# Attention in a hybrid decoder layer: turning two steps behind the scores instead of one

## The chip, the cores and the metric

One core of a Trainium2 chip runs one layer of a decoder trunk in float32. The metric is the device time of one execution in microseconds (us), lower is better. TensorE is PE in the profile (its weight loads PEld), VectorE is DVE, ScalarE is ACT, GpSimd is POOL, and SyncE (SP) issues nearly all transfers.

## The reference

The layer normalises x (2048 rows of 1024), scales and shifts it by an adaptive modulation, projects it once, and feeds three token mixers: spatial gating, an mLSTM matrix memory, and stick-breaking attention. Their outputs are gated, concatenated, projected and added to x. The change lies in the attention, with 6 heads of 64 and blocks of 128 queries:

```python
z = jnp.einsum('bthd,bshd->bhts', qb, kb).astype(jnp.float32) * scale
strict = s_idx[None, :] < t_idx[:, None]
log_not = jnp.where(strict, jax.nn.log_sigmoid(-z), 0.0)
suffix = lax.cumsum(log_not, axis=3, reverse=True) - log_not
a = jnp.where(strict, jnp.exp(jax.nn.log_sigmoid(z) + suffix), 0.0)
outs.append(jnp.einsum('bhts,bshd->bthd', a.astype(vb.dtype), vb))
```

Each weight is sigmoid(z) times the product of all 1 - sigmoid(z) at later keys.

## The kernel before

**Blocks and passes.** The 16 query tiles of 128 rows are taken in three blocks of 5, 5 and 6. For each block the attention runs in three passes p, each of two heads. `c_proj` makes the pass's queries, keys and values (`Qst`, `Kst`, `Vst`), then `stick` yields the attention step by step, and `interleave` sets matmuls of the other projections (`bqk_proj`, `bg_proj`, `cz_proj`, `a_proj`; here "filler") between the steps by their cost. Behind the third pass comes `bv_proj` (tiles `pv`). After the last block an output stage reads everything back, runs the mLSTM and the output projection.

**A unit** is one query tile i, one head h and up to 512 keys from tile s0 on. It passes four functions. `front` (L372) makes the scores z with two matmuls (L378, L379); ACT evacuates them twice, sigmoid(-z) into `bb` (L383) and sigmoid(z) into `be` (L384); POOL masks the tile on the diagonal (L386, L388); VectorE scans `bb` from the right into running products (L391); and VectorE for every other unit, POOL for the rest, multiplies `be` by them (L395). `middle` (L399) turns `be` by up to four transposes on TensorE into the PSUM tile `at` (L406), ACT copies that into `aT` (L408), and VectorE subtracts the rounded copy to get the remainder (L409, here "the subtraction"). `back` (L413) multiplies by the values (L421, the products) and at a row's end adds the two halves (L425 on ACT, L427 on VectorE). `fin` (L431) folds two heads into a tile and stores it (L437 to L440). A scan takes its start from the scan of the unit before it in the same row (`carry`).

**Order.** The loop at the end of `stick` takes unit n's front, then the middle of unit n-1, the back of n-2, the fin of n-3:

```python
        for n in range(N + 3):
            for lag, fn in ((0, front), (1, middle), (2, back), (3, fin)):
                if 0 <= n - lag < N:
                    yield fn(units[n - lag])
```

This is the order in which the steps are handed to a scheduler, which then places every instruction on its engine's queue by priority (attention stands ahead of filler, `STK` = -30) and by its own estimate of when inputs are there. What it leaves is one fixed order per engine, and each engine works its queue in that order. There are 240 units.

**Tiles.** In SBUF the pool `stk` holds 4 tiles of `bb`, 3 of `be` and 3 of `aT` (4 KB a partition). `aT` also serves two tiles of x at the start (L120), `be` two rows of norm weights (L212). In PSUM the scores have 2 banks, `at` 2, the products 1, the projections 3.

Of the kernel before, what the change touches and what calls it, by code (L numbers as in the profile page):

```python
# [8 lines left out]
F32 = mybir.dt.float32  # L9
F32R = mybir.dt.float32r  # L10
# [7 lines left out]
P = 128  # L18
SEQ = 2048
NT = SEQ // P  # L20
D = 1024
# [11 lines left out]
def hybrid_block_kernel(ctx: ExitStack, tc: tile.TileContext, x, c, norm_g, w_ada, b_ada, w_in,  # L33
                        ga_v_norm, ga_ws, ga_bs, mb_conv_w, mb_conv_b, mb_b_i, mb_b_f, mb_h_norm,
                        sc_q_norm, sc_k_norm, w_out, out):
    nc = tc.nc
# [59 lines left out]
    stk = rs.enter_context(tc.tile_pool(name="stk", bufs=2, side="right"))  # L96
# [18 lines left out]
    def load_x(i, j, halves=None):  # L115
        if halves is None:
            if j % 4 < 2:
                xt = tmp.tile([P, D], F32, tag="xt", name=f"xt{i}")
            else:
                xt = stk.tile([P, D], F32, tag="aT", bufs=3, name=f"xt{i}")  # L120
            nc.sync.dma_start(xt, x[0, i * P:(i + 1) * P, :])
            xtiles[i] = [[xt], None]
        else:
            for hh in range(2):
                nc.sync.dma_start(halves[hh], x[0, i * P:(i + 1) * P, hh * 512:(hh + 1) * 512])
            xtiles[i] = [halves, None]
# [27 lines left out]
    def get_x(i, j):  # L154
        load_x(i, j % 2)
        rms_x(i)
        for hh in range(len(xtiles[i][0])):
            w = D // len(xtiles[i][0])
            mod_x(i, hh * w, (hh + 1) * w)
# [49 lines left out]
    brow = [stk.tile([P, 512], F32, tag="bb", bufs=4, name=f"brow{n}") for n in range(4)]  # L209
    for n in (2, 0, 3, 1):  # L210
        nc.gpsimd.memset(brow[n], 0.0)
    g_bc = [stk.tile([P, 512], F32, tag="be", bufs=3, name=f"g_bc{n}") for n in range(2)]  # L212

    def ada_load(half):
        for n, c0 in enumerate((1024 + 512 * half, 512 * half)):
# [43 lines left out]
    for j in range(NB0):  # L259
        halves = None  # L260
        if j == 4:
            halves = vg_halves(4)
        elif j == 5:
            halves = [t512(f"x5_{hh}") for hh in range(2)]
        load_x(j, j, halves)
        if j < 2:
            staged[j] = load_w(w_in[0], c_segs(0), j)
# [89 lines left out]
    def stick(p, t0, nb):  # L357
# [14 lines left out]
        def front(u):  # L372
            i, j, h, s0, s1 = u
            w = (s1 - s0) * P
            nm = f"{p}_{i}_{h}_{s0}"
            z = pz.tile([P, 512], F32, tag="z", name=f"z{nm}")
            kk = Kst[:, h, s0 * P:s1 * P]
            nc.tensor.matmul(z[:, :w], lhsT=Qst[:, j, 0, h, :], rhs=kk, start=True, stop=False)  # L378
            nc.tensor.matmul(z[:, :w], lhsT=Qst[:, j, 1, h, :], rhs=kk, start=False, stop=True)  # L379
            bb = stk.tile([P, 513], F32, tag="bb", bufs=4, name=f"bb{nm}")  # L380
            be = stk.tile([P, 512], F32, tag="be", bufs=3, name=f"be{nm}")
            nc.gpsimd.memset(bb[:, w:w + 1], 1.0)  # L382
            nc.scalar.activation(bb[:, :w], z[:, :w], AF.Sigmoid, scale=-1.0)  # L383
            nc.scalar.activation(be[:, :w], z[:, :w], AF.Sigmoid)  # L384
            if s1 == i + 1:
                nc.gpsimd.affine_select(out=bb[:, w - P:w], in_=bb[:, w - P:w], pattern=[[-1, P]],  # L386
                                        compare_op=ALU.is_gt, fill=1.0, base=0, channel_multiplier=1)
                nc.gpsimd.affine_select(out=be[:, w - P:w], in_=be[:, w - P:w], pattern=[[-1, P]],  # L388
                                        compare_op=ALU.is_gt, fill=0.0, base=0, channel_multiplier=1)
            rev = bb[:, 0:w + 1][:, ::-1]  # L390
            nc.vector.tensor_tensor_scan(rev, rev, rev, carry.get((i, h), 1.0), ALU.mult, ALU.bypass)  # L391
            carry[i, h] = bb[:, 0:1]
            eng = nc.gpsimd if len(st_count) % 2 else nc.vector
            st_count.append(0)
            eng.tensor_tensor(be[:, :w], be[:, :w], bb[:, 1:w + 1], ALU.mult)  # L395
            st[u] = [be, None]
            return 2 * w / 2.4

        def middle(u):  # L399
            i, j, h, s0, s1 = u  # L400
            nm = f"{p}_{i}_{h}_{s0}"
            be = st[u][0]
            nb_ = s1 - s0
            at = pat.tile([P, 4, P], F32, tag="at", name=f"at{nm}")
            for s in range(nb_):
                nc.tensor.transpose(at[:, s, :], be[:, s * P:(s + 1) * P], ident)  # L406
            aT = stk.tile([P, 4, 2, P], F32R, tag="aT", bufs=3, name=f"aT{nm}")
            nc.scalar.copy(aT[:, :nb_, 0, :], at[:, :nb_, :])  # L408
            nc.vector.tensor_tensor(aT[:, :nb_, 1, :], at[:, :nb_, :], aT[:, :nb_, 0, :].bitcast(F32), ALU.subtract)  # L409
            st[u][1] = aT  # L410
            return nb_ * 109
# [29 lines left out]
            return 430  # L441

        N = len(units)
        for n in range(N + 3):
            for lag, fn in ((0, front), (1, middle), (2, back), (3, fin)):
                if 0 <= n - lag < N:
                    yield fn(units[n - lag])

# [595 lines left out]
```

## Time and profile before

| | |
|---|---|
| median of 3 runs | 1482.28 us (1481.29 to 1483.16) |
| the profiled execution, its own time | 1480.27 us |
| its span, first to last instruction | 1478.5 us |
| mean granted TensorE clock | 0.982 of full speed |
| busy: PE, PEld | 1400.6 us, 1302.7 us |
| busy: DVE, ACT, POOL | 1025.1 us, 678.1 us, 647.3 us |
| DMA moved | 233.19 MB, mean 158 GB/s |

Busy time is what an engine spends in instructions. "Idle before" is time in which it stood still just ahead of an instruction, and the name behind the arrow is what ended that. Times of matmuls include a modelled end, so back-to-back matmuls overlap in the listing. All windows below are us from the span's start.

### The profile page before, as it was taken

Reading aid. Unit: us, or ns where it says so; the run is one execution under the profiler, and the core shown is the slowest. Engines: PE = TensorE matmul, PEld = TensorE weight load, DVE = VectorE, ACT = ScalarE, POOL = GpSimd, SP = SyncE. Lnnn points to the kernel's source line nnn. Section 1 sums busy time; section 2 is a strip of 40 time slices with the busy share of each in tenths; the row PEclk is TensorE's granted clock in tenths of the full one; section 3 lists DMA queues with packets and bytes.
Section 4 is the critical chain, followed back from the end, with each engine's and each line's share of the span. In section 5 each row is a group of like instructions: output and inputs, shape, how many; then the busy total and the mean of one; then the engine's idle time right before and its main releaser. Section 6 shows DMA issues by size and latency. Waiting matters only on the chain.

```text
span 1478.5 us, 24942 instructions
## 1 busy us (share of the span) xinstructions
PE 1400.6 (95%) x8468; PEld 1302.7 (88%) x8468; DVE 1025.1 (69%) x1778; ACT 678.1 (46%) x1656; POOL 647.3 (44%) x1140
## 2 busy tenths in 40 slices
PE   4999999889999999999999899999999978999998
PEld 3789999879999999988899799989999867888887
DVE  6796555586894566588698975778778888444443
ACT  3365444444464355446367655555455655211210
POOL 4463554573443433455233353433344336534442
PEclk9999999999999999999999999999999998999999
DMA  9866766657635534625332343303432524555551
GB/s 319 305 203 216 249 213 190 207 187 240 203 114 194 175 114 137 213 98 184 114 117 78 104 148 131 104 27 107 158 100 74 190 89 128 185 152 159 171 156 57
DMA packets 187103, 233.19 MB, mean 158 GB/s; under 512 B 22714, under 2 KB 160344, under 8 KB 186976
## 3 DMA queue, kind: packets, MB, share of 16 engines
q1 hardware_dynamic: 186752, 231.59, 48.1%
q8 instruction: 67, 1.10, 0.3%
q14 instruction: 60, 0.49, 0.1%
q0 software_dynamic: 224, 0.02, 0.0%
HBM read 159.24 MB, written 72.31 MB: 157 GB/s over the span
## 4 chain that ended last, share of the span: by engine, by line
PE 68%; DVE 16%; DMA 5%; issue 4%; POOL 3%; ACT 3%; SPq 1%; DVEq 0%; POOLq 0%; ACTq 0%
DVE bb L391 6%; PE av L421 5%; PE pc L296 4%; PE pc L298 4%; PE at L406 4%; PE pc L297 4%; PE po L957 4%; PE po L959 3%; PE po L958 3%; PE pg L298 3%; PE pg L297 3%; PE pg L296 3%; PE pb L465 2%; PE pb L464 2%; PE z L378 2%
## 5 line engine op out<-in xcount | busy, mean ns | idle before, releaser
L391 DVE TENSOR_TENSOR_SCAN bb<-bb,bb 128x513 f32<-128x513 f32 x144 | 194.1, 1348 | 24.9 <-ACT bb L383 23.8
L395 POOL TENSOR_TENSOR be<-be,bb 128x512 f32<-128x512 f32 (+3 forms) x120 | 133.0, 1108 | 148.3 <-DVE bb L391 69.2
L409 DVE TENSOR_TENSOR aT<-at,aT 128x512 fp32r<-128x512 f32 (+3 forms) x240 | 142.7, 597 | 31.5 <-ACT aT L408 30.5
L421 PE MATMUL av<-aT,Vst 128*128 128x256 f32 x816 | 146.4, 296 | 15.0 <-DVE aT L409 12.1
L408 ACT CAST aT<-at 128x512 fp32r<-128x512 f32 (+3 forms) x240 | 127.1, 530 | 70.3 <-PE at L406 67.4
L383 ACT ACTIVATE bb<-z 128x512 f32<-128x512 f32 (+3 forms) x240 | 130.3, 544 | 54.5 <-PE z L379 44.2
L421 PEld LDWEIGHTS av<-aT,Vst 128*128 128x128 f32 x816 | 120.5, 192 | 27.0 <-DVE aT L409 19.2
L296 PE MATMUL pc<-wr,hT 128*128 128x384 f32 (+1 forms) x384 | 136.8, 358 | 7.6 <-DVE hT L290 5.7
L406 PE MATMUL at<-ident,be 128*128 128x128 f32 x816 | 132.8, 277 | 9.6 <-DVE Qst L351 4.5
L298 PE MATMUL pc<-wr,hT 128*128 128x384 f32 (+1 forms) x384 | 135.5, 353 | 1.6 <-DVE hT L290 1.5
L297 PE MATMUL pc<-wr,hT 128*128 128x384 f32 (+1 forms) x384 | 134.0, 349 | 0.0
L384 ACT ACTIVATE be<-z 128x512 f32<-128x512 f32 (+3 forms) x240 | 132.1, 550 | 0.0
L406 PEld LDWEIGHTS at<-ident,be 128*128 128x128 f32 x816 | 99.2, 142 | 19.0 <-DVE aT L409 8.0
L957 PE MATMUL po<-wo,yT 128*128 128x512 f32 x256 | 105.0, 410 | 0.3 <-ACT yT L946 0.3
L958 PE MATMUL po<-wo,yT 128*128 128x512 f32 x256 | 102.3, 400 | 1.9 <-DVE wo L864 1.9
L391 DVE TENSOR_TENSOR_SCAN bb<-bb 128x129 f32<-128x129 f32 (+3 forms) x96 | 86.9, 905 | 23.5 <-POOL bb L386 16.3
L959 PE MATMUL po<-wo,yT 128*128 128x512 f32 x256 | 101.5, 400 | 0.0
L382 POOL MEMSET bb<- 128x1 f32 x240 | 24.2, 101 | 168.4 <-DVE bb L391 118.1
L378 PE MATMUL z<-Kst,Qst 128*128 128x512 f32 (+3 forms) x240 | 92.7, 387 | 1.7 <-ACT be L384 1.6
L466 PE MATMUL pb<-hT,wr 128*128 128x320 f32 (+1 forms) x288 | 91.9, 324 | 2.4 <-DVE wr L190 2.4
L464 PE MATMUL pb<-hT,wr 128*128 128x320 f32 (+1 forms) x288 | 93.1, 324 | 0.6 <-DMA wr<-w_d 0.6
L465 PE MATMUL pb<-hT,wr 128*128 128x320 f32 (+1 forms) x288 | 92.2, 322 | 0.0
(272 smaller groups left out, 3905.2 us busy)
## 6 DMA issues: line engine op xcount, KB each, us to landing
wr<-w_d SPq DMA_DIRECT2D x160, 384.0 KB, 5.6
w_d<-wr SPq DMA_DIRECT2D x80, 384.0 KB, 3.5
wad<-in_w_ada_dram SPq DMA_DIRECT2D x8, 1024.0 KB, 6.8
xo<-in_x_dram SPq DMA_DIRECT2D x16, 512.0 KB, 3.7
out_dram<-o SPq DMA_DIRECT2D x31, 256.0 KB, 2.9
xt<-in_x_dram SPq DMA_DIRECT2D x15, 512.0 KB, 3.5
st<-in_w_in_dram SPq DMA_DIRECT2D x60, 128.0 KB, 3.7
wr<-w_d SPq DMA_DIRECT2D x16, 392.0 KB, 6.0
```

The source lines that it names most:

```text
L296: nc.tensor.matmul(ps, lhsT=hT[:, 0, k, cols], rhs=wt[k][:, 0, :W], start=k == 0, stop=False)
L297: nc.tensor.matmul(ps, lhsT=hT[:, 0, k, cols], rhs=wt[k][:, 1, :W], start=False, stop=False)
L298: nc.tensor.matmul(ps, lhsT=hT[:, 1, k, cols], rhs=wt[k][:, 0, :W], start=False, stop=k == KT - 1)
L384: nc.scalar.activation(be[:, :w], z[:, :w], AF.Sigmoid)
L391: nc.vector.tensor_tensor_scan(rev, rev, rev, carry.get((i, h), 1.0), ALU.mult, ALU.bypass)
L395: eng.tensor_tensor(be[:, :w], be[:, :w], bb[:, 1:w + 1], ALU.mult)
L406: nc.tensor.transpose(at[:, s, :], be[:, s * P:(s + 1) * P], ident)
L409: nc.vector.tensor_tensor(aT[:, :nb_, 1, :], at[:, :nb_, :], aT[:, :nb_, 0, :].bitcast(F32), ALU.subtract)
L421: nc.tensor.matmul(flat(av), lhsT=Vst[:, s0 + s, h, :], rhs=flat(aT[:, s]), start=(s0 + s == i), stop=(s0 + s == 0))
L957: nc.tensor.matmul(po, lhsT=yT[:, 0, k, :], rhs=wo[k][:, 0, cs], start=k == 0, stop=False)
L958: nc.tensor.matmul(po, lhsT=yT[:, 0, k, :], rhs=wo[k][:, 1, cs], start=False, stop=False)
L959: nc.tensor.matmul(po, lhsT=yT[:, 1, k, :], rhs=wo[k][:, 0, cs], start=False, stop=k == KT - 1)
```

## The change

The middle of a unit is queued two steps behind its front, the back three, the fin four. The tags `be` and `aT` get a fourth tile each. To make room in SBUF the program's DMA scratch is set to 4096 bytes.

```diff
-                xt = stk.tile([P, D], F32, tag="aT", bufs=3, name=f"xt{i}")
+                xt = stk.tile([P, D], F32, tag="aT", bufs=4, name=f"xt{i}")
...
-    g_bc = [stk.tile([P, 512], F32, tag="be", bufs=3, name=f"g_bc{n}") for n in range(2)]
+    g_bc = [stk.tile([P, 512], F32, tag="be", bufs=4, name=f"g_bc{n}") for n in range(2)]
...
-            be = stk.tile([P, 512], F32, tag="be", bufs=3, name=f"be{nm}")
+            be = stk.tile([P, 512], F32, tag="be", bufs=4, name=f"be{nm}")
...
-            aT = stk.tile([P, 4, 2, P], F32R, tag="aT", bufs=3, name=f"aT{nm}")
+            aT = stk.tile([P, 4, 2, P], F32R, tag="aT", bufs=4, name=f"aT{nm}")
...
-        for n in range(N + 3):
-            for lag, fn in ((0, front), (1, middle), (2, back), (3, fin)):
+        for n in range(N + 4):
+            for lag, fn in ((0, front), (2, middle), (3, back), (4, fin)):
...
-    nc = _bacc.Bacc("TRN2", target_bir_lowering=False, num_devices=1)
+    nc = _bacc.Bacc("TRN2", target_bir_lowering=False, num_devices=1, dynamic_dma_scratch_size=4096)
```

Since the scheduler places everything anew, the order on each engine moves in many places. Names in the rows that follow read pass, query tile, head, first key tile, running number: `bb2_2_1_0_3609` is pass 2, tile 2, head 1, keys from tile 0 on.

VectorE, first block, third pass, from the subtraction of the first unit to the scan of the third tile's second head. Before:

```order
L409 TENSOR_TENSOR aT2_0_0_0_3478<-at2_0_0_0_3476,aT2_0_0_0_3478 128x128
L543 TENSOR_TENSOR tb1_0_3587<-pa1_0_3458,ta1_0_3586 128x384
L391 SCALAR_TENSOR_TENSOR bb2_2_0_0_3547<-bb2_2_0_0_3547 128x385
L539 TENSOR_SCALAR ta1_1_3690<-ta1_1_3690 128x256
L409 TENSOR_TENSOR aT2_0_1_0_3500<-at2_0_1_0_3498,aT2_0_1_0_3500 128x128
L540 TENSOR_TENSOR ta1_1_3690<-pa1_1_3602,ta1_1_3690 128x256
L548 TENSOR_REDUCE rra1_0_3596<-ta1_0_3586 128x2
L395 TENSOR_TENSOR be2_2_0_0_3548<-be2_2_0_0_3548,bb2_2_0_0_3547 128x384
L427 TENSOR_TENSOR avt2_0_0_3510<-av2_0_0_3506,avs2_0_0_3508 128x128
L391 SCALAR_TENSOR_TENSOR bb2_2_1_0_3609<-bb2_2_1_0_3609 128x385
```

The same place with the change:

```order
L409 TENSOR_TENSOR aT2_0_0_0_3495<-at2_0_0_0_3493,aT2_0_0_0_3495 128x128
L543 TENSOR_TENSOR tb1_0_3601<-pa1_0_3458,ta1_0_3600 128x384
L539 TENSOR_SCALAR ta1_1_3698<-ta1_1_3698 128x256
L391 SCALAR_TENSOR_TENSOR bb2_2_0_0_3532<-bb2_2_0_0_3532 128x385
L391 SCALAR_TENSOR_TENSOR bb2_2_1_0_3564<-bb2_2_1_0_3564 128x385
L409 TENSOR_TENSOR aT2_0_1_0_3517<-at2_0_1_0_3515,aT2_0_1_0_3517 128x128
L540 TENSOR_TENSOR ta1_1_3698<-pa1_1_3616,ta1_1_3698 128x256
```

The scan of tile 2, head 1 moved ahead of the subtraction of tile 0, head 1.

TensorE, last block, third pass, from the last projection matmul (L298) on. Before:

```order
L298 MATMUL pv15_14742<-wr33_7_14595,hT_130 128x384
L421 MATMUL av2_13_0_13885<-aT2_13_0_12_13853,Vst_444 128x256 x2
L437 MATMUL py2_12_13888<-fold_79,avt2_12_1_13862 128x64
L378 MATMUL z2_13_1_4_13995<-Kst_443,Qst_126 128x512
L379 MATMUL z2_13_1_4_13995<-Kst_443,Qst_126 128x512
L406 MATMUL at2_13_0_4_13907<-ident_74,be2_13_0_4_13868 128x128 x4
```

With the change:

```order
L298 MATMUL pv15_14742<-wr33_7_14595,hT_130 128x384
L378 MATMUL z2_13_1_8_13953<-Kst_443,Qst_126 128x512
L379 MATMUL z2_13_1_8_13953<-Kst_443,Qst_126 128x512
L421 MATMUL av2_12_1_13794<-aT2_12_1_0_13840,Vst_444 128x256 x4
L406 MATMUL at2_13_0_8_13887<-ident_74,be2_13_0_8_13829 128x128 x4
L437 MATMUL py2_12_13901<-fold_79,avt2_12_0_13768 128x64
L378 MATMUL z2_13_1_4_13978<-Kst_443,Qst_126 128x512
L379 MATMUL z2_13_1_4_13978<-Kst_443,Qst_126 128x512
```

One unit's scores, one turning and one product group that stood ahead of the last projection matmul stand behind it.

VectorE, the end of the attention, from the last scan but one. Before:

```order
L391 SCALAR_TENSOR_TENSOR bb2_15_1_4_14480<-bb2_15_1_4_14480,bb2_15_1_8_14451 128x513
L409 TENSOR_TENSOR aT2_15_0_0_14438<-at2_15_0_0_14433,aT2_15_0_0_14438 128x4x128
L395 TENSOR_TENSOR be2_15_1_4_14481<-be2_15_1_4_14481,bb2_15_1_4_14480 128x512
L391 SCALAR_TENSOR_TENSOR bb2_15_1_0_14506<-bb2_15_1_0_14506,bb2_15_1_4_14480 128x513
L409 TENSOR_TENSOR aT2_15_1_12_14463<-at2_15_1_12_14458,aT2_15_1_12_14463 128x4x128
```

With the change:

```order
L391 SCALAR_TENSOR_TENSOR bb2_15_1_4_14461<-bb2_15_1_4_14461,bb2_15_1_8_14436 128x513
L409 TENSOR_TENSOR aT2_15_0_4_14423<-at2_15_0_4_14418,aT2_15_0_4_14423 128x4x128
L391 SCALAR_TENSOR_TENSOR bb2_15_1_0_14490<-bb2_15_1_0_14490,bb2_15_1_4_14461 128x513
L395 TENSOR_TENSOR be2_15_1_4_14462<-be2_15_1_4_14462,bb2_15_1_4_14461 128x512
L409 TENSOR_TENSOR aT2_15_0_0_14448<-at2_15_0_0_14443,aT2_15_0_0_14448 128x4x128
```

The last scan stands one subtraction earlier, so five subtractions follow it instead of four.

## Rows read from the trace of the kernel before

**Rows 1.** The page, part 1: busy us (share of the span) and instructions.

```profile
PE 1400.6 (95%) x8468; PEld 1302.7 (88%) x8468; DVE 1025.1 (69%) x1778; ACT 678.1 (46%) x1656; POOL 647.3 (44%) x1140
```

**Rows 2.** Waits of PE, 50 to 1160 us: us in total, times, longest us.

```profile
PE av L421 <- DVE aT L409: 5.1, 5, 3.0
PE at L406 <- DVE Qst L351: 4.5, 2, 3.2
...
PE at L406 <- DVE aT L409: 2.6, 5, 0.7
...
PE py L437 <- DVE aT L409: 2.4, 3, 1.2
...
PE av L421 <- DVE avt L427: 1.6, 3, 0.9
PE z L378 <- ACT be L384: 1.0, 3, 0.6
```

**Rows 3.** Busy us (instructions) by stretch: PE, PEld, DVE, ACT, POOL, PEclk, DMA, GB/s.

```profile
298.00:303.00 5.00, 2.04 (x10) 1.48 (x9) 4.55 (x7) 1.07 (x5) 3.97 (x6) 0.66 0.54 185
303.00:310.00 7.00, 6.99 (x31) 6.62 (x31) 6.68 (x18) 4.39 (x15) 5.98 (x14) 0.76 0.35 106
806.00:824.00 18.00, 14.13 (x88) 11.11 (x87) 16.19 (x24) 12.68 (x29) 9.06 (x17) 1.00 0.02 5
1166.00:1214.00 48.00, 36.83 (x224) 29.59 (x222) 43.54 (x55) 31.11 (x66) 18.72 (x35) 0.93 0.49 180
```

**Rows 4.** Waits of PE, 1160 to 1214 us, the last stretch.

```profile
PE av L421 <- DVE aT L409: 6.9, 8, 1.6
PE at L406 <- DVE aT L409: 1.4, 2, 1.2
PE py L437 <- DVE aT L409: 1.1, 2, 0.7
```

**Rows 5.** Timelines of PE and DVE: start us, us, instruction [idle before <- releaser].

```profile
245.48 0.74 PE L421 MATMUL av<-aT,Vst 128*128 128x256 f32 x4 [0.31 <-DVE aT L409]
...
302.15 0.58 PE L421 MATMUL av<-aT,Vst 128*128 128x256 f32 x1 [2.96 <-DVE aT L409]
303.02 0.95 DVE L391 TENSOR_TENSOR_SCAN bb<-bb 128x385 f32<-128x385 f32 x1
...
813.07 2.67 DVE L391 TENSOR_TENSOR_SCAN bb<-bb,bb 128x513 f32<-128x513 f32 x2
816.37 0.74 PE L421 MATMUL av<-aT,Vst 128*128 128x256 f32 x4 [1.29 <-DVE aT L409]
...
1042.75 0.43 PE L437 MATMUL py<-fold,avt 128*128 128x64 f32 x2 [0.40 <-DVE aT L409]
...
1212.16 0.69 DVE L409 TENSOR_TENSOR aT<-at,aT 128x512 fp32r<-128x512 f32 x1 [1.47 <-ACT aT L408]
```

**Rows 6.** Costliest groups, whole span: busy us, mean ns | idle before us <- releasers.

```profile
L391 DVE TENSOR_TENSOR_SCAN bb<-bb,bb 128x513 f32<-128x513 f32 x144 | 194.1, 1348 | 24.9 <-ACT bb L383 23.8
...
L409 DVE TENSOR_TENSOR aT<-at,aT 128x512 fp32r<-128x512 f32 (+3 forms) x240 | 142.7, 597 | 31.5 <-ACT aT L408 30.5
...
L384 ACT ACTIVATE be<-z 128x512 f32<-128x512 f32 (+3 forms) x240 | 132.1, 550 | 0.0
...
L408 ACT CAST aT<-at 128x512 fp32r<-128x512 f32 (+3 forms) x240 | 127.1, 530 | 70.3 <-PE at L406 67.4 <-DVE aT L409 1.9
...
L382 POOL MEMSET bb<- 128x1 f32 x240 | 24.2, 101 | 168.4 <-DVE bb L391 118.1 <-PE pada L232 27.4 <-DVE be L395 20.7
```

**Rows 7.** The last stretch, 1160 to 1214 us: groups of DVE, by form.

```profile
L391 DVE TENSOR_TENSOR_SCAN bb<-bb,bb 128x513 f32<-128x513 f32 x15 | 20.9, 1393 | 0.6 <-ACT bb L383 0.5
L409 DVE TENSOR_TENSOR aT<-at,aT 128x512 fp32r<-128x512 f32 x20 | 13.3, 672 | 3.3 <-ACT aT L408 3.2
```

**Rows 8.** Timeline of POOL at the start of the program.

```profile
7.00 0.34 POOL L470 COPY xb<-halo 128x3 f32<-128x3 f32 x1
14.25 0.10 POOL L382 MEMSET bb<- 128x1 f32 x1 [6.92 <-PE pada L232]
```

## The prediction

> **What bounds the kernel now.** I read the page's shares first, then who waits for whom on TensorE, then the stretches in which TensorE is not full. TensorE is busy 95% of the span and VectorE 69% [rows 1]: the reader sees an engine that is nearly full, so a change that adds or removes no matmul can gain only from its idle time. The waits of TensorE before the last stretch of the attention, from 50 to 1160 us, show whose idle time that is [rows 2]. Those with an attention matmul on the left are the products and turnings that wait for the subtraction of L409 (5.1 + 2.6 + 2.4 us, 13 waits), the small sum L427 (1.6 us), the evacuation of the scores L384 (1.0 us), and a pass's first turnings that wait for a Qst (4.5 us, start of a pass, not of a unit). What the reader has to look for is missing: no attention matmul there waits for the scan L391 or the product L395, the two that stand between the scores and the turning.
>
> Two stretches are different. From 806 to 824 us TensorE is busy 14.13 of 18 us and VectorE 16.19; from 1166 to 1214, where the projections have run out and attention is alone, TensorE 36.83 of 48 and VectorE 43.54 [rows 3]. There VectorE sets the pace, and TensorE waits for L409 in 6.9 + 1.4 + 1.1 us [rows 4]. From 298 to 303 us VectorE is busy 4.55 of 5 us and TensorE 2.04 [rows 3]: one wait of 2.96 us for a subtraction [rows 5].
>
> **The change, part by part.** *The later turning.* Nothing is added or taken away: 240 units with the same instructions, the same bytes. What the change buys is time between a unit's scores and its turning: in the order on TensorE the median distance from the first score matmul to the first turning is 57 to 86 matmuls before and 66 to 113 after, by pass; from the turning to the products it is 27 to 62 before and 22 to 60 after, so the second distance does not grow. The scan and the multiplication get more time, the subtraction none. Since no wait of TensorE ends on the first two [rows 2], what it gains directly is 0.
>
> *The subtraction behind more scans.* VectorE works in its written order, and with scores one unit further ahead a further scan stands ahead of some subtractions. In the third pass of the first block, the second subtraction now has the scan of unit (2, head 1) ahead of it, and had not before. A scan of this width, 385 columns, took 0.95 us a moment after the wait [rows 5], a full one 1.35 us [rows 6]. The wait of 2.96 us itself stands as it was, for the rows ahead of the first subtraction are the same but for two swapped. The Trainium skill, page "TensorE: Matmul & The Clock Gate", section on the array of 32x32 sub-arrays, says that VectorE's queue is strictly first in, first out; this trace agrees (two scans run from 813.07 to 815.74, the subtraction only then, and the products start at 816.37 [rows 5]); by that rule alone every wait of rows 2 on L409 would grow by a scan, where I count one.
>
> The bounds: above, the 8 separate places into which the 13 waits fall (the first at 245 us, the last at 1042 us [rows 5]) each grow by one full scan, 8 x 1.35 = 10.8 us. Below, a scan that runs earlier may fall into idle time of VectorE (31% of the span [rows 1]) and shorten the queue later: all of 5.1 + 2.6 + 2.4 = 10.1 us go [rows 2]. I take one narrow scan exposed, **+0.95 us**, since the one place whose order I can follow to the wait shows exactly that.
>
> *The last stretch.* After the last projection matmul the order leaves 19 units of scores to issue where it left 18, and that matmul stands 11 matmuls earlier. One unit more costs VectorE a scan and a subtraction, 1.39 + 0.67 = 2.06 us [rows 7]; its multiplication lies on POOL every second time and is left out. The 11 matmuls of TensorE that moved behind the point are about a unit's worth: at the stretch's own pace, 224 matmuls in 36.83 us [rows 3], 11 x 0.16 = 1.8 us by which the stretch starts earlier. Net +0.3 us. Against it, in the drain behind the last scan VectorE stands idle 1.47 us for the copy of the last turning [rows 5], and now five subtractions instead of four stand behind that scan, so one of 0.67 us can fill idle time: -0.7. The two nearly cancel, and I put **0**; bounds -1.5 (that idle time filled) and +2.1 (a whole unit more).
>
> *The added tiles.* A fourth tile for the products (tag be) and for the turned products (aT). ACT's evacuation L384, which would wait for a tile of be, was never idle ahead of it (0.0 us), and L408 of 70.3 us idle had 67.4 for the turning itself [rows 6]: no wait for these tiles shows, so **0**. Without them, two steps could not stand in line. The tag bb keeps its 4 tiles, and there POOL waits 118.1 us for a scan to give one back [rows 6]; what stands behind that wait on POOL is the mask and every other multiplication. Here the cover is the distance to the turning, which grows. The Trainium skill, page "Perfetto Trace Analysis", section "Optimization Strategy", says that a gap repeating on the engine that should be full can mean too few buffers; by that rule the two added tiles would win back what TensorE waits in the attention; the rows say its repeating gap is L409, which no tile of these two holds up.
>
> *The DMA scratch.* Smaller by the new argument, to make room. It serves the seven small parameter loads that POOL issues near the start (L244 to L249); behind them POOL is idle for 6.92 us, until 14.25 [rows 8], which covers a delay of theirs, and all later transfers are issued by SP. **0**, bounds 0 and a few us.
>
> *SP, ACT.* On SP some stores and loads change places with a neighbour or two, the loads of x by one place at most; 0.
>
> **Sum.** 0.95 + 0 + 0 + 0 = +0.95 us on the profiled execution's 1480.27, so 1481.2. The median of the runs, 1482.28, lies 2.0 us above that execution; on it the forecast is **1483.2 us**. A measurement of this kernel can tell some 0.2%, 3 us, from no change; the forecast is no change.
>
> **Rivals.** *The subtraction becomes the bound (slower).* Place: VectorE's queue wherever it is nearly full, as at 806 and at 843 to 847 us. Price: at half of the 8 places a full scan, 4 x 1.35 = +5.4 us, 1487.7 us; up to 10.8. It decides as soon as a subtraction's products stand on TensorE within one scan's time behind it. For it: all the waits of rows 2 that belong to a unit end on L409 or behind it. Against it: VectorE has 31% idle, and the scans run earlier may use it.
>
> *Room between scores and turning smooths VectorE (faster).* With scores a unit ahead, VectorE has a scan to do where it now waits for a copy. Price: half to all of the 10.1 us of L409 waits, and with the wait at 302 us goes the low clock behind it: granted 0.66 and 0.76 from 298 to 310 [rows 3], a mean of times at 1.2 and at 2.4 GHz; 7 us at 0.76 instead of 1 are 1.7 us. That gives -5.1 to -11.8, so 1477.2 to 1470.5 us. For it: rows 2 are really waits inside the attention. Against it: the distance from turning to products does not grow, and the place at 302 us is as it was.
>
> *Buffers were short (faster).* If the tiles of be and aT were what held the units up, the waits for L409 outside and inside the last stretch would go, 10.1 + 6.9 + 1.4 + 1.1 = 19.5 us: 1462.8 us [rows 2, 4]. L384's 0.0 us idle [rows 6] speaks against it. This is what the rule of "Perfetto Trace Analysis" in the Trainium skill, cited above, would come to here.
>
> *The change does nothing.* The scheduler places by its own estimate and the last stretch already ran scores three units ahead of turnings, four after; the time then is 1482.3, inside the forecast.
>
> **Chances.** No change, with the last of these, 0.45; the subtraction as the bound 0.26, of which 0.23 is slower by over 0.2% and 0.03 within; smoothing 0.25, short buffers 0.02; the scratch or a reordered load that hurts 0.02. Splitting the same way: faster by over 0.2% 0.27, within 0.48, slower 0.25. The range that leaves out no more than 2 in 10 takes three quarters of the 10.1 us below, 1482.3 - 7.6 = 1474.7, and two thirds of the 10.8 above, 1482.3 + 7.2 = 1489.5.
>
> **What would show it.** Right: TensorE's waits for L409 between 50 and 1160 us come to about 10 to 12 us again, the wait near 302 us is still there, the last projection matmul ends near 1164 and the last products near 1213 us. The slower rival: the same waits at 15 us or more with scans right ahead of the subtractions. The faster: those waits at half, VectorE's idle time behind L408 (30.5 us over the span [rows 6]) clearly smaller. The forecast falls if a load of weights or x takes a new wait of over 3 us, or if the time of the last stretch, 48 us, moves by more than 3.

## The result and the profile after

The change makes the kernel slower: 1491.81 us against 1481.85 us in the same session (medians of 5 runs each), ratio 1.0076, 95% interval 1.0062 to 1.0091. The forecast was no change, 1483.2 us, range 1474.7 to 1489.5; the result lies above the range. The profiled execution took 1492.14 us, span 1490.4.

The page of the changed kernel, part 1, answers to [rows 1]; below it the group of the products:

```profile
PE 1402.5 (94%) x8468; PEld 1306.6 (88%) x8468; DVE 1028.7 (69%) x1778; ACT 677.8 (45%) x1656; POOL 661.0 (44%) x1140
...
L421 PE MATMUL av<-aT,Vst 128*128 128x256 f32 x816 | 148.0, 297 | 26.2 <-DVE aT L409 16.2
```

The same group in the kernel before:

```profile
L421 PE MATMUL av<-aT,Vst 128*128 128x256 f32 x816 | 146.4, 296 | 15.0 <-DVE aT L409 12.1
```

The instructions are the same in number, TensorE is busy 2 us longer, and the span grew by 11.9 us. Idle time is what grew, most of all ahead of the products (L421): 26.2 us where it was 15.0. Who ended that idle time is in the waits of PE from 50 to 1160 us, which answer to [rows 2]:

```profile
PE av L421 <- DVE avt L427: 7.1, 7, 2.7
PE av L421 <- DVE aT L409: 6.5, 9, 3.2
PE at L406 <- DVE Qst L351: 4.4, 2, 3.2
...
PE pb L464 <- DMA wr<-w_d: 2.5, 2, 2.2
PE at L406 <- DVE m0C L695: 2.1, 1, 2.1
PE at L406 <- DVE g_row L602: 2.0, 1, 2.0
...
PE at L406 <- DVE aT L409: 1.8, 2, 1.3
```

Products now wait 7.1 us for L427, the add at a row's end, where they waited 1.6. That add empties the one PSUM tile of the products, so the next row's first products stand behind it. The waits for the subtraction L409 have not grown in sum: those of products from 5.1 to 6.5 us, the others have shrunk. From 1160 to 1223 us the products wait longer than in [rows 4]:

```profile
PE av L421 <- DVE aT L409: 9.7, 11, 1.5
PE av L421 <- DVE avt L427: 2.8, 4, 1.4
```

The second of these rows, before, from 1160 to 1214 us:

```profile
PE av L421 <- DVE avt L427: 1.0, 1, 1.0
```

How such a wait comes about is seen on VectorE and ScalarE near the last of them, where TensorE waits 1.40 us (timeline of ACT, then of DVE; start us, us, instruction, idle before):

```profile
1198.32 0.29 ACT L425 COPY avs<-av 128x128 f32<-128x128 f32 x1
```

```profile
1197.49 0.56 DVE L409 TENSOR_TENSOR aT<-at,aT 128x384 fp32r<-128x384 f32 x1 [0.53 <-ACT aT L408]
1199.05 1.29 DVE L391 TENSOR_TENSOR_SCAN bb<-bb 128x513 f32<-128x513 f32 x1 [1.00 <-POOL bb L386]
1200.26 0.26 DVE L427 TENSOR_TENSOR avt<-av,avs 128x128 f32<-128x128 f32 x1
```

ScalarE's half was copied at 1198.61, but the add ran at 1200.26: ahead of it in VectorE's queue stood the scan of a later unit, which itself had to wait 1.00 us for POOL's mask.

Set against the marks of the program, the 11.9 us fall into three parts. The last projection matmul (pv) starts at 1169.66 instead of 1164.04 us: +5.6. From it to the last product of the attention: 53.4 instead of 49.3 us, +4.1. From there to the last product of the output projection (tiles po): 262.5 instead of 260.3, +2.2. The windows of the changed kernel, with the last stretch as it lies now, answer to [rows 3]:

```profile
298.00:303.00 5.00, 1.79 (x9) 1.47 (x8) 4.55 (x8) 1.26 (x5) 4.03 (x8) 0.80 0.42 144
303.00:310.00 7.00, 7.00 (x28) 6.68 (x28) 7.00 (x16) 4.38 (x13) 5.33 (x13) 0.65 0.36 111
806.00:824.00 18.00, 15.22 (x96) 12.72 (x96) 14.07 (x22) 12.21 (x28) 5.07 (x13) 1.00 0.02 5
1170.00:1223.20 53.20, 39.99 (x248) 32.60 (x247) 46.47 (x57) 33.78 (x71) 19.35 (x36) 0.94 0.47 164
```

One profile is no exact measure of these parts. Of each order there are three profiles up to the output stage, for some of the runs below keep it until there. In the order of before (before, e3_scratch, f4_pad_b) the last projection matmul stands at 1164.0, 1160.3 and 1166.3 us, and the last stretch takes 49.3, 51.6 and 49.4. In the order of the change (the change, f1_be4, k1_wodve_a) it stands at 1169.7, 1171.3 and 1169.4, and the stretch takes 53.4, 53.3 and 54.9. The two orders do not overlap in either, but a single pair of profiles can be wrong by several us.

### The profile page after: what moved, and what is told of

Its sections match the earlier page's. It is cut to its first block, busy times and chain, and to the rows that moved or that the text cites. A ratio compares the mean times of both kernels' runs of the same rounds, so it can differ in the third digit from the quotient of the medians.

```text
span 1490.4 us, 24992 instructions
## 1 busy us (share of the span) xinstructions
PE 1402.5 (94%) x8468; PEld 1306.6 (88%) x8468; DVE 1028.7 (69%) x1778; ACT 677.8 (45%) x1656; POOL 661.0 (44%) x1140
## 4 chain that ended last, share of the span: by engine, by line
PE 73%; DVE 12%; issue 5%; DMA 4%; POOL 3%; ACT 3%; SPq 1%; DVEq 0%; POOLq 0%; ACTq 0%
PE av L421 5%; PE at L406 4%; DVE bb L391 4%; PE pc L296 4%; PE pc L298 4%; PE pc L297 4%; PE po L959 4%; PE po L957 4%; PE po L958 4%; PE pg L296 3%; PE pg L297 3%; PE pg L298 3%; PE z L378 2%; PE z L379 2%; PE pb L464 2%
## 5 line engine op out<-in xcount | busy, mean ns | idle before, releaser
L421 PE MATMUL av<-aT,Vst 128*128 128x256 f32 x816 | 148.0, 297 | 26.2 <-DVE aT L409 16.2
L409 DVE TENSOR_TENSOR aT<-at,aT 128x512 fp32r<-128x512 f32 (+3 forms) x240 | 142.1, 598 | 30.1 <-ACT aT L408 29.4
L421 PEld LDWEIGHTS av<-aT,Vst 128*128 128x128 f32 x816 | 120.4, 191 | 42.2 <-DVE aT L409 24.1
L298 PE MATMUL pc<-wr,hT 128*128 128x384 f32 (+1 forms) x384 | 135.6, 353 | 1.4 <-DVE hT L290 1.3
L384 ACT ACTIVATE be<-z 128x512 f32<-128x512 f32 (+3 forms) x240 | 131.9, 549 | 0.0
```

What stands on the lines that cost most here:

```text
L298: nc.tensor.matmul(ps, lhsT=hT[:, 1, k, cols], rhs=wt[k][:, 0, :W], start=False, stop=k == KT - 1)
L421: nc.tensor.matmul(flat(av), lhsT=Vst[:, s0 + s, h, :], rhs=flat(aT[:, s]), start=(s0 + s == i), stop=(s0 + s == 0))
```

## The experiments

Each was timed against the kernel before, which took 1479.7 to 1480.7 us in these sessions; the ratio of the change is that of its own session, against 1481.85. The table has one profile each: "ahead" is how many units' scores TensorE has issued beyond the one being subtracted, mean over the 240 subtractions, counted from the timelines; "L427" is PE's wait of products for that add over the whole span; then the start of the last pv matmul, the last stretch from it to the last product of the attention, and the output stage from there to the last output product, all us.

| run | lag, be, aT, priority | ratio (95%) | median | ahead | L427 | last pv matmul | last stretch | output |
|---|---|---|---|---|---|---|---|---|
| before | 1, 3, 3, -30 | 1 | 1479.9 | 3.33 | 2.6 | 1164.0 | 49.3 | 260.3 |
| e3_scratch | 1, 3, 3, -30 | 0.9992 (0.9982 to 1.0002) | 1478.5 | 3.34 | 2.6 | 1160.3 | 51.6 | 258.6 |
| e2_lag | 2, 3, 3, -30 | 0.9979 (0.9967 to 0.9990) | 1477.4 | 3.41 | 1.6 | 1163.5 | 47.1 | 258.3 |
| f2_aT4 | 2, 3, 4, -30 | 0.9983 (0.9969 to 0.9997) | 1477.3 | 3.41 | 2.6 | 1163.3 | 49.2 | 259.7 |
| i_l20 | 2, 3, 3, -20 | 1.0000 (0.9988 to 1.0013) | 1480.3 | 3.41 | 2.1 | 1167.8 | 47.1 | 259.4 |
| i_l60 | 2, 3, 3, -60 | 1.0018 (1.0006 to 1.0030) | 1482.7 | 3.47 | 3.5 | 1161.3 | 51.2 | 259.4 |
| e1_tiles | 1, 4, 4, -30 | 1.0052 (1.0037 to 1.0067) | 1487.8 | 3.99 | 11.0 | 1164.6 | 54.0 | 262.6 |
| the change | 2, 4, 4, -30 | 1.0076 (1.0062 to 1.0091) | 1491.8 | 4.14 | 9.9 | 1169.7 | 53.4 | 262.5 |
| f1_be4 | 2, 4, 3, -30 | 1.0069 (1.0048 to 1.0090) | 1489.9 | 4.15 | 10.3 | 1171.3 | 53.3 | 258.9 |
| h3_lag3_be4 | 3, 4, 3, -30 | 1.0074 (1.0054 to 1.0095) | 1490.6 | 4.24 | 11.8 | 1168.7 | 54.0 | 259.4 |
| i_a20 | 2, 4, 4, -20 | 1.0110 (1.0095 to 1.0125) | 1497.0 | 4.08 | 12.4 | 1172.0 | 54.9 | 263.0 |
| i_a60 | 2, 4, 4, -60 | 1.0002 (0.9991 to 1.0014) | 1480.7 | 4.20 | 4.5 | 1158.3 | 53.3 | 262.6 |
| j_a60_aT3 | 2, 4, 3, -60 | 0.9981 (0.9968 to 0.9993) | 1477.3 | 4.22 | 5.8 | 1158.7 | 54.3 | 260.1 |
| g3_lag1_be2 | 1, 2, 3, -30 | 1.0066 (1.0047 to 1.0085) | 1489.5 | 2.59 | 8.7 | 1165.4 | 60.1 | 260.6 |
| g1_lag2_be5 | 2, 5, 3, -30 | 1.0108 (1.0072 to 1.0144) | 1495.6 | 4.70 | 12.7 | 1185.2 | 47.1 | 258.7 |

### Which part of the change costs

The scratch alone, the tiles alone, the later turning alone, starting from the kernel before:

```diff
e3_scratch
+    nc = _bacc.Bacc("TRN2", ..., dynamic_dma_scratch_size=4096)
e1_tiles
+    as e3_scratch, and bufs=4 for the tags "be" and "aT"
e2_lag
-        for n in range(N + 3):
-            for lag, fn in ((0, front), (1, middle), (2, back), (3, fin)):
+        for n in range(N + 4):
+            for lag, fn in ((0, front), (2, middle), (3, back), (4, fin)):
```

e3_scratch: 

> The kernel before with the 4096 bytes of DMA scratch alone; its order of instructions is that of the kernel before on every engine. If the scratch has no part in the slowdown: 1482, within 3 us, and the same waits at the same places as in the rows of the kernel before to 0.5 us. If the smaller scratch delays POOL's DMA issues: most of the 10 us, 1488 to 1492, and POOL's first DMA waits well after 14 us.

e1_tiles: 

> The change without the later turning: fourth be and aT tiles and the small scratch, but lags of 1, 2, 3 steps as before. Theory A (the later turning itself costs: products come later and more of them meet the one PSUM tile of the row that is being emptied): 1482, within 3 us, PE's wait of products for L427 at 2 to 4 us. Theory B (any new order costs, since the scheduler places all else anew): a shift of 3 us or more in either direction, with waits in new places. Theory C (the tiles themselves cost): 1488 to 1492.

e2_lag: 

> The later turning alone, with three be and three aT tiles and the scratch as before. Theory A (the later turning costs by the one products tile): 1489 to 1494, products waiting for L427 at 8 us or more. Theory B (new order): anywhere from 1480 to 1495, and the wait for L427 not above 5 us. Theory C (the tiles cost): 1482 to 1485.

The scratch costs nothing. The tiles alone bring the ratio to 1.0052, and the later turning alone gains a little, 0.9979, which is faster than any of the three theories had it. Theory A falls: the step that gives the change its name is not what makes it slow. The waits of products show it, first with the later turning alone, then with the tiles alone:

```profile
PE av L421 <- DVE aT L409: 6.7, 7, 2.9
...
PE av L421 <- DVE avt L427: 1.6, 3, 0.7
```

```profile
PE av L421 <- DVE aT L409: 15.5, 17, 3.2
PE av L421 <- DVE avt L427: 11.0, 11, 2.7
```

Then each added tile alone, with the later turning:

```diff
f1_be4
+    as e2_lag and e3_scratch, and bufs=4 for the tag "be"
f2_aT4
+    as e2_lag and e3_scratch, and bufs=4 for the tag "aT"
```

f1_be4: 

> Later turning and the small scratch with a fourth tile for products (be) alone; aT has three. Theory D (three be tiles were a brake that kept the scores at most three units ahead of the turning; the fourth lets scores and scans in front of the work that ends a row, so that the rows' adds and the last stretch come later): 1489 to 1494, products waiting for L427 8 us or more, last stretch from the last projection product to the last product of the attention 53 us or more. Rival E (the fourth aT tile does it, because more turned units stand in front of the row's end): 1476 to 1480 and the wait for L427 under 3 us.

f2_aT4: 

> Later turning and the small scratch with a fourth tile for turned products (aT) alone; be has three. Its order of instructions is that of the run with the later turning alone. Theory D: 1475 to 1480, as that run, waits the same to 0.5 us. Rival E: 1487 or more. If the place of the tiles in memory costs by itself: above 1481 with unchanged order.

With the fourth aT tile no engine's order differs from that of e2_lag, and the time is that of e2_lag, a second measurement of its small gain. Its waits were expected to be the same to 0.5 us and are not: products wait 8.7 us for the subtraction and 2.6 for the add, where e2_lag has 6.7 and 1.6, so that much is chance from one profile to the next. The fourth be tile alone takes the ratio from 0.9979 to 1.0069, some 13 us. Theory D stands here, E falls.

### Is it the number of be tiles?

```diff
g1_lag2_be5
+    as f1_be4 with bufs=5 for the tag "be"
g3_lag1_be2
+    the kernel before with the small scratch and bufs=2 for the tag "be"
h3_lag3_be4
-        for n in range(N + 3):
-            for lag, fn in ((0, front), (1, middle), (2, back), (3, fin)):
+        for n in range(N + 5):
+            for lag, fn in ((0, front), (3, middle), (4, back), (5, fin)):
+    and bufs=4 for the tag "be", the small scratch
```

g1_lag2_be5: 

> Later turning, small scratch, five be tiles and three aT tiles. Theory D (a brake taken off): no better than the changed kernel, 1490 or more, the wait for L427 and the last stretch at least as long as there (9.9 us and 53 us). Rival B (each new order is a lottery of its own): anywhere from 1475 to 1495, not ordered by the number of be tiles.

g3_lag1_be2: 

> The kernel before with two be tiles and the small scratch, turning one step behind. Theory D taken to its end: the brake is harder, the wait for L427 under 2.6 us, the last stretch no longer than 50 us, but scores now wait for the turning of two units before (new waits of scores or of the activations into be); time 1478 to 1490. Rival B: any change of order, with waits in new places, 1475 to 1495.

h3_lag3_be4: 

> Turning queued three steps behind the scores, four be tiles, three aT tiles, small scratch. If what counts is the number of be tiles (theory D): 1488 to 1494, as with four tiles at one and two steps. Rival F (what counts is how many tiles there are beyond those that the lag fills; here one beyond, as in the run with two steps and three tiles): 1475 to 1482.

What sets how far the scores run ahead is the number of be tiles, as the column "ahead" has it: 2.59 with two be tiles, 3.33 to 3.47 with three, 3.99 to 4.24 with four, 4.70 with five; at three tiles the second step of lag moves it from 3.33 to 3.41 only. A unit's score cannot be evacuated before a be tile is free, and the scheduler respects that when it writes the order. With the priority number at -30 three tiles were the best of the counts that were run, two to four at one step of lag (four with the fourth aT tile) and three to five at two, and h3_lag3_be4 excludes F. Two expectations of theory D missed: with two tiles the wait for L427 rose to 8.7 us and the last stretch to 60.1 instead of falling, and with five tiles the last stretch was 47.1 instead of 53 or more; the time there was lost earlier, the last pv matmul standing at 1185.2.

### Is the late add the cause, or a sign?

```diff
e6_avhalves_a (from the changed kernel)
-                acc[i, h] = pav.tile([P, 4, P], F32, tag="av", name=f"av{p}_{i}_{h}")[:, 0:2, :]
+                acc[i, h] = avs2[0][:, 2 * h:2 * h + 2, :]
...
+        avs2 = [pav.tile([P, 4, P], F32, tag="av", name=f"av{p}_{t0}")]
e5_actevac_a (from the changed kernel)
-                t1 = stk.tile([P, P], F32, tag="avs", name=f"avs{p}_{i}_{h}")
-                nc.scalar.copy(t1, av[:, 1, :])
+                t1 = stk.tile([P, 2, P], F32, tag="avs", bufs=1, name=f"avs{p}_{i}_{h}")
+                nc.scalar.copy(t1, av)
...
-                nc.vector.tensor_tensor(t2, av[:, 0, :], t1, ALU.add)
+                nc.gpsimd.tensor_tensor(t2, t1[:, 0, :], t1[:, 1, :], ALU.add)
```

e6_avhalves_a: 

> The changed kernel, but the two heads of a stage use the two halves of one PSUM tile in turn for their products, so that a row's first products need not wait until the row before has been emptied. Theory A (the one products tile): PE's wait of products for L427 falls from 9.9 us to under 2, and the time from 1491.8 to 1482 to 1486. Theory B (new order, loads at the block changes and the last stretch): the wait for L427 falls as well, but the time stays within 3 us of 1491.8, since other waits come last there.

e5_actevac_a: 

> The changed kernel, but ScalarE copies both halves of a row's products out of PSUM and GpSimd adds them in SBUF, so that the one products tile comes free without VectorE. Theory D1 (the loss comes through the add L427, which stands behind scans on VectorE): PE's wait of products for the add (9.9 us) is gone, what is left of it on ScalarE's copy is under 4 us, and the time is 1480 to 1486. Rival D2 (the late add is one sign of a crowded VectorE, and what it held is held by the next late thing): the wait moves to the copy, to the subtraction (L409) or to the sums of a row (L437), and the time stays within 3 us of 1491.8.

e6_avhalves_a took 1495.1 us, 1.0099 (1.0083 to 1.0115), and told nothing about the question: the wait stayed, 10.4 us in 11 places, and each of them ended with the add of the row just before, which lies in the other half. In this program two halves of one PSUM tile are one thing to wait for. e5_actevac_a did take the wait away and was no faster, 1495.3 us, 1.0103 (1.0088 to 1.0119). Its waits of products:

```profile
PE av L421 <- DVE aT L409: 22.2, 21, 3.2
...
PE av L421 <- ACT avs L425: 0.3, 1, 0.3
```

The 9.9 us are gone and the subtraction has taken 6 of them over, from 16.2 to 22.2. D2 stands for the wait, though the time lies 3.5 us above 1491.8 and not within its 3: the add is one of several things that stand late in VectorE's queue. In e5_actevac_a the last stretch is short, 48.2 us, but the last pv matmul stands at 1178.8, so its time is lost earlier. As a mark of a slow order the wait for the add serves all the same: in the table every kernel with 5.8 us or less of it takes up to 1482.7 us, every one with 8.7 or more at least 1487.8. (Moving the add also gave GpSimd 96 more instructions, so this run is not the removal of a wait alone.)

### Is it the tile, or the order that came of it?

The attention's priority number sets how the scheduler ranks it; another number gives all engines another order without any other change.

```diff
i_a60, i_a20 (from the changed kernel); i_l60, i_l20 (from e2_lag)
-STK = -30
+STK = -60
...
+STK = -20
```

i_a60: 

> The changed kernel with the attention's priority number at -60 instead of -30 (nothing else), which gives the scheduler's order another shake on all engines. Theory D: still 1486 to 1496, 8 us or more above the next run. Rival B (each order is a lottery of its own): anywhere from 1475 to 1495, and not reliably above the next run.

i_l60: 

> The later turning alone (three be and three aT tiles) with the attention's priority number at -60 instead of -30. Theory D: 1474 to 1483, 8 us or more under the run with four tiles and the same priority number. Rival B: anywhere from 1475 to 1495.

i_a20: 

> The changed kernel with the attention's priority number at -20 instead of -30 (the rest as in the changed kernel). Theory D (the fourth be tile costs in nearly every order, -60 was the exception): 1487 to 1496 and 7 us or more above the next run. Rival B (the order is a lottery): 1476 to 1496, and less than 7 us above the next run or under it.

i_l20: 

> The later turning alone (three be, three aT tiles) with the attention's priority number at -20. Theory D: 1474 to 1484. Rival B: 1475 to 1495, not reliably under the run with four tiles and the same number.

At -60 the four tiles cost nothing against before and are 2 us under three tiles; at -20 they cost 16.7 us more than three. So theory D in its plain form falls too: the tile has no fixed price. What the runs show is a wider spread, 1480.7 to 1497.0 us over three orders, against 1477.4 to 1482.7 with three tiles; three orders each are few to call that a rule. At -60 the scores run just as far ahead (4.20), but the waits of products are these:

```profile
PE av L421 <- DVE aT L409: 10.9, 16, 1.5
PE z L378 <- ACT be L384: 6.2, 5, 4.5
PE av L421 <- DVE avt L427: 4.5, 8, 1.4
```

The last pv matmul then stands at 1158.3 us, 11 us earlier than in the changed kernel. The last stretch is the one part that four tiles lengthened in every order: 53.3 to 54.9 us in nine profiles with the add on VectorE, 47.1 to 51.6 in eight with three. (The eight and nine include runs told further on.) Behind the last pv matmul 23 subtractions are left in all nine, 21 to 23 in the eight.

### The output stage

The column "output" parts the runs in another way: 262.5 us or more where both tiles were added, at most 260.6 where one or none was. In this stage yT holds the mixed rows, turned for the output projection, and wo the weights of that projection; each is split into a rounded copy and its remainder, which a subtraction makes. Both added tiles together take 6 KB a partition, and with them the scheduler puts VectorE's first two subtractions into yT behind six of the splits of wo (L864) instead of ahead of them. A tile of that size that nothing uses does the same to the kernel before; the reverse takes the second tile out at -60.

```diff
f4_pad_b (from the kernel before, with the small scratch)
+    pad = stk.tile([P, 1536], F32, tag="pad", bufs=1, name="pad")
j_a60_aT3 (from i_a60)
-                xt = stk.tile([P, D], F32, tag="aT", bufs=4, name=f"xt{i}")
+                xt = stk.tile([P, D], F32, tag="aT", bufs=3, name=f"xt{i}")
...
-            aT = stk.tile([P, 4, 2, P], F32R, tag="aT", bufs=4, name=f"aT{nm}")
+            aT = stk.tile([P, 4, 2, P], F32R, tag="aT", bufs=3, name=f"aT{nm}")
```

f4_pad_b: 

> The kernel before with the small scratch and one tile of 6 KB that nothing uses, beside the attention's tiles. Its order is that of the kernel before up to the last stage, where the subtractions into yT fall behind seven of the splits of wo on VectorE, as in the changed kernel. Theory G (the added memory by itself moves this order, and that costs): from the last product of the attention to the last output product 262 to 263 us instead of 258.5 to 260.5, products po waiting about 7 us for yT, the time 1482 to 1486. Rival (the order there costs nothing, since the products are only shifted): 1479 to 1481.

j_a60_aT3: 

> The changed kernel with the priority number at -60 and three aT tiles instead of four. Only the order of the last stage differs from the run with -60 and both added tiles. Theory G: 1475 to 1479, 2 to 5 us under that run's 1480.7, and from the last product of the attention to the last output product 258 to 260 us instead of 262.6. Rival: 1480 to 1482.

f4_pad_b took 1485.7 us, 1.0027 (1.0014 to 1.0039), with 263.4 us of output stage; j_a60_aT3 0.9981 where i_a60 had 1.0002. In these two orders the 6 KB cost 4 and 3 us. In the change's own order the same comparison is f1_be4, whose order is that of the changed kernel up to the output stage: there it is 3.7 us shorter in the profile, but the ratio is only 0.0007 lower (1.0069 for 1.0076), 1 us, and the intervals are wider than that. How much of the change's loss is this is therefore not settled: it lies between nothing and some 5 us. The wait expected at the products po was elsewhere in f4_pad_b, where products of the mLSTM (tiles c) wait for kw, which VectorE makes at L650:

```profile
PE c L921 <- DVE kw L650: 9.0, 1, 9.0
```

In the changed kernel it is at po. Behind both stands a single VectorE instruction; timelines of the changed kernel, of DVE, of POOL and of PE:

```profile
1241.18 8.02 DVE L864 TENSOR_TENSOR wo<-wst,wo 128x512 fp32r<-128x512 f32 x1
1249.20 0.68 DVE L947 TENSOR_TENSOR yT<-pty,yT 128x512 fp32r<-128x512 f32 x1
```

```profile
1240.81 1.14 POOL L923 TENSOR_TENSOR C<-C,decay 96x388 f32<-96x388 f32 x1
1241.91 3.69 POOL L864 TENSOR_TENSOR wo<-wst,wo 128x512 fp32r<-128x512 f32 x3
1245.57 0.62 POOL L637 TENSOR_SCALAR_AFFINE_SELECT wT<-wT 128x512 f32<-128x512 f32 x1
1246.17 2.47 POOL L864 TENSOR_TENSOR wo<-wst,wo 128x512 fp32r<-128x512 f32 x2
```

```profile
1249.93 0.80 PE L959 MATMUL po<-wo,yT 128*128 128x512 f32 x1 [7.91 <-DVE yT L947]
```

A split that takes 0.68 us elsewhere takes 8.02 here, as long as POOL runs without a pause, to 1248.64. The kernel before has the same hold:

```profile
1232.21 7.14 DVE L653 SCALAR_TENSOR_TENSOR sm<-nd,ex 128x4 f32<-128x4 f32 x1
```

but with yT made early TensorE has output products to do for most of it (busy 12.00 of the 12 us from 1224 to 1236, 6.60 of the 8 from 1232 to 1240). In all 18 profiles in which GpSimd does half of the splits, one VectorE instruction behind the attention takes 7.1 to 8.1 us. The Trainium skill, page "SBUF — State Buffer", section "SBUF: two separate sides", says that VectorE and GpSimd share one pair of ports under an exclusive lock: of a VectorE instruction with two inputs in SBUF and a GpSimd instruction that reads SBUF, the one that starts first has it for the whole instruction, and the other is blocked. The trace agrees that one is held, but here VectorE stands back while seven GpSimd instructions run on end, not one. Taking the splits off GpSimd tests it:

```diff
k1_wodve_a (from the changed kernel), k2_wodve_lag (from e2_lag)
-        (nc.gpsimd if k % 2 else nc.vector).tensor_tensor(wo[k][:, 1, cs], src, wo[k][:, 0, cs].bitcast(F32),
+        nc.vector.tensor_tensor(wo[k][:, 1, cs], src, wo[k][:, 0, cs].bitcast(F32),
```

k1_wodve_a: 

> The changed kernel, but all splits of wo on VectorE and none on GpSimd (eight more of 0.7 us there at the start of the last stage). Theory H (VectorE is held while GpSimd runs without a pause, and the hold stands in the path): no VectorE instruction of 3 us or more after 1223 us, from the last product of the attention to the last output product 257 to 261 us instead of 262.6, the time 1486 to 1490. Rival (the order of the splits before yT costs, whoever does them; 5.5 us more of them on VectorE): 263 us or more, 1492 to 1497.

k2_wodve_lag: 

> The later turning alone (three be, three aT tiles), with all splits of wo on VectorE. Theory H: there TensorE has output products during the hold, so little is gained: 1474 to 1479, from the last product of the attention to the last output product 256 to 260 us (258.3 with GpSimd's splits). Rival: 1480 or more, since VectorE gets 5.5 us more in the last stage.

The splits on VectorE, count and duration min/median/max in ns, in the changed kernel and in k1_wodve_a:

```profile
L864 DVE TENSOR_TENSOR wo<-wst,wo x8: 654/684/8017, 1232.4 to 1252.0; 128x512 fp32r<-128x512 f32 x8
```

```profile
L864 DVE TENSOR_TENSOR wo<-wst,wo x16: 654/678/1427, 1233.3 to 1247.8; 128x512 fp32r<-128x512 f32 x16
```

k1_wodve_a took 1488.1 us, 1.0052 (1.0034 to 1.0070), with 257.8 us of output stage: twice the splits on VectorE, none over 1.43 us, and the stage 4.7 us shorter. Twelve splits stand ahead of yT there instead of six, and yet the first subtraction into it starts 20.4 us after the last product of the attention instead of 26.2, which speaks against the rival, the order of the splits. Theory H stands, with the reservation that the order of that stage moved as well; and the gain in time, 0.0024 of the ratio, is hardly more than the two intervals allow. k2_wodve_lag took 1471.57 us, 0.9945 (0.9929 to 0.9960), and is **faster than both kernels**; its output stage is 257.2 us. It gained more against e2_lag than H had expected. The hold was not fully covered there: PE waited 3.2 us at po for a split of wo, a wait that is gone. But the output stage is only 1.1 us shorter than e2_lag's and 2.5 shorter than f2_aT4's, which has the same order, while the ratio fell by 0.0034, 5 us; the rest of the gain is not accounted for.

## Why the prediction was wrong

*The later turning: 0.* Right in size: alone it measures 0.9979 and 0.9983, at the edge of what can be told from no change. At the other priority numbers it measures 1.0000 and 1.0018 against the kernel before at -30, so a gain in general is not shown. Wrong in what it was credited with: the longer distance from score to turning comes mostly from the be tiles, not from the lag ("ahead" 3.41 with the lag alone, 3.99 with the tiles alone).

*The subtraction behind more scans: +0.95.* The waits for L409 from 50 to 1160 us went from 10.1 [rows 2] to 8.8 us (6.5 + 1.8 + 0.5), inside the bounds but under the 10 to 12 that were to show it right (in the trace the 13 waits before fall into nine places at least 20 us apart, not eight, which would have raised the upper end of the range by 0.9 us only); the one near 302 us is still there, 3.2 instead of 2.96. At the place from which the +0.95 was taken, the second subtraction behind one more scan, nothing was exposed: TensorE is busy 7.00 of the 7 us from 303 to 310. The argument was right about the queue and looked at one instruction in it: a scan that moves ahead delays whatever stands behind it, and that was the add L427. Its 1.6 us stood in [rows 2] and got no term; 7.1 stand there now.

*The last stretch: 0, bounds -1.5 to +2.1.* It measured +4.1, past the 3 us at which the prediction gave itself up. The unit more was counted rightly (23 subtractions for 22; the last projection matmul stands 12 matmuls earlier in the trace, not 11, which changes little), but it was cancelled against an idle time that was not filled (1.29 us ahead of the last subtraction, 1.47 before); the waits for the add in the stretch (2.8 us for 1.0) were not thought of.

*The added tiles: 0.* **This is the step that failed.** It was argued from L384, never idle for want of a be tile [rows 6]. That was true and proved nothing: a tile count is a limit that the scheduler keeps when it writes the order, so scores are placed where a tile is free and no wait is left to see. In place of the 0, the fourth be tile let the scores run 4.15 units ahead instead of 3.41 and took the ratio from 0.9979 to 1.0069 (f1_be4 against e2_lag), some 13 us in the order at -30; that more than makes up the whole loss. For the fourth aT tile by itself the 0 was right (f2_aT4). "Without them, two steps could not stand in line" was false as well: e2_lag runs two steps with three tiles.

*DMA scratch, SP: 0.* Right (e3_scratch). But the memory for which the scratch made room moved the order of the output stage, in a part of the program that the prediction did not look at: 4 us in f4_pad_b.

*The rivals.* The time, +10 us, is near the slower rival's upper end, +10.8, but that is chance and not its mechanism: the waits for the subtraction outside the last stretch did not grow. Nor did they halve, as the faster rival, smoothing, would have had it. "Buffers were short" had the sign of the tiles reversed: by the rule that the prediction cites from the Trainium skill, page "Perfetto Trace Analysis", section "Optimization Strategy", the added tiles would have won time; the runs differ from it, for the fourth be tile lost time in every order but those at -60, and the fourth aT tile alone changed nothing.

What stays open: why the orders at -20 and -30 with four tiles reach the last projection matmul 6 to 14 us later than the one at -60. The waits name the add and the subtraction, and removing one only moved it to the other. The loss of 10 us is thus shown to come with the fourth be tile in the order at -30 (1.0069 of 1.0076 without the fourth aT tile); which place of that order costs it is not shown, nor how much the 6 KB add to it. The kernel before was not run at the other priority numbers, nor with all splits on VectorE.

## What to carry to other kernels

Under a scheduler that fixes the order, a buffer count is a brake on how far one step runs ahead, and the trace of before shows no wait for it: try the counts one by one, and not only upwards. Before a step is credited or blamed, shake the order by something that should not matter; here that moved the four-tile kernel by 16 us, more than the change itself. When GpSimd and VectorE share a burst of two-input work, look for one VectorE instruction many times its usual length and for what stands behind it; giving all of it to one engine made the fastest version.

## What the runs showed of the hardware that was not expected

A VectorE instruction on 128x4 elements took 7.14 us in the kernel before, and a 0.68 us one took 8.02 in the changed kernel, each ending within 0.6 us of the end of an unbroken run of GpSimd instructions. Such a hold of 7.1 to 8.1 us stands in all 18 profiles with GpSimd's splits, now on one instruction, now on another, even in one and the same order (7.14 us at L653 in the kernel before, 8.13 at L864 in e3_scratch); in the two profiles without them no VectorE instruction behind the attention took over 1.47 us. And 6 KB a partition that no instruction touches cost 0.27% (0.14 to 0.39) with a changed order of the output stage, while the 4 KB of f2_aT4 left the order as it was and cost nothing.
